# Linear attention: the norms of the small tokens divided at each wait of TensorE and dealt at half tiles, the next weights requested ahead of a norm

## The chip and the metric

The kernel runs on one NeuronCore of a Trainium2 chip. The engines are called here as the profile calls them: PE (TensorE: matmuls and transposes), DVE (VectorE), ACT (ScalarE), POOL (GpSimd) and SP (SyncE, whose queue issues most of the transfers). Each engine takes its own instructions in the order in which the built program lists them, and waits at semaphores for the others. The metric is the device time of one execution in microseconds (us), as the median of several runs.

## What is computed

One inference step of a two-layer decoder: a layer of gated linear attention (GLA), then one of differential attention, each followed by an MLP. There is a prompt of 1024 tokens, and beside it a few small tokens: 16 meta tokens and 8 samples, which the kernel keeps as one block of 32 columns. The change lies in the first layer, where the small tokens go through the whole layer beside the prompt's projections:

```python
def post_norm(x, f, g, b):
    return layer_norm(DEEPNORM_ALPHA * x + f, g, b)

def sq_relu_mlp(x, w1, w2):
    h = jax.nn.relu(x @ w1)
    return (h * h) @ w2
...
    q, k, v, lg, r = gla_project(x, w_in, w_gate, b_gate)
    s_new, o = gla_chunk(state.astype(F32), q, k, v, lg)
    return gla_output(o, r, g_norm, w_out, x.dtype), s_new
...
        x_s = post_norm(x_s, f_s, ln_mix_g[layer], ln_mix_b[layer])
...
        x_s = post_norm(x_s, sq_relu_mlp(x_s, mlp_w1[layer], mlp_w2[layer]), ln_mlp_g[layer], ln_mlp_b[layer])
```

## The kernel before

The prompt is held as high and low float32r parts, so one product is three matmuls (`mm3`, lines 206 to 208). For the heads 1 to 3, `proj(h)` (line 370) makes q, k (four tiles of 24 matmuls) and v (four tiles of 48); `decays` (435) makes the decay factors, the 32x32 blocks of At and the transposed keys (487); `advance` (494) takes a chunk's four blocks through the state (500 to 502 on PE, 504 on DVE). Then come the gates r of all heads (line 842 on), and w_out of this layer.

The small tokens are a generator beside it, `small_tokens` (779). `s_rows` (702) and `s_cols` (715) multiply by a weight matrix in pieces: two weight tiles of 1 MB are requested (lines 234 and 240, into two buffers, `swt`), then a `yield`, then 8 thin matmuls (712, 723), which the profile counts twice. The matrices come in this order: w_out of the attention, the two halves of the first MLP weight, the second MLP weight (8 pieces), and the input weight of the next layer (four pieces and two). `s_post` (726) follows w_out and the second MLP weight: an eviction by ACT (731), four transposes (734), the sum with x on DVE (740, 741), then `s_ln` (744): a sum over the columns (746), an average by a matmul (748), the subtraction (749), squares and their sum (751, 752), a second average (754), a logarithm and an exponential on ACT (758, 759), and small DVE steps up to 767.

`deal()` (819) takes the generator one `yield` further. It is called at each second tile of `proj`, at some chunks of `decays`, and once for each half of a gate tile (863), 25 times in all, so that the whole `s_post` stands between two calls.

What runs when isn't set by this order alone: the program is built by a scheduler which lists each engine's instructions by its own reckoning of what is ready, with the order of the code as the priority. The decode of the second layer (cache pages, lines 906 to 943) is code of a lower priority, which starts as soon as the small tokens' q and k rows are written.

Of the kernel before, what the change touches and what calls it, by code (L numbers as in the profile page):

```python
# [21 lines left out]
P = 128  # L22
D = 1024
T = 1024
NB = 8
# [89 lines left out]
def hybrid_step(ctx, tc, A, dbg=None, upto=9):  # L115
# [227 lines left out]
    ps = smt()  # L343
# [26 lines left out]
    def proj(h):  # L370
        hi, lo = qku if h == 0 else qk_unit(h)
        hv, lv = (w.rearrange("p (i k n) -> p i k n", i=2, n=P) for w in (hi, lo))
        for c in range(h == 0, 2):
            cs = slice(512 * c, 512 * c + 512)
            for i in range(2):
                ps = mmt()
                for k in range(NB):
                    mm3(ps, hv[:, i, k, :], lv[:, i, k, :], XH[:, k, cs], XL[:, k, cs], k == 0, k == NB - 1)
                evict_qk(c, i, ps)
                yield  # L380
        hi, lo = v0u if h == 0 else kunit(wi, 1024 + h * 256)
        hv, lv = (w.rearrange("p (k n) -> p k n", n=256) for w in (hi, lo))
        for c in range(2):
            for i2 in range(2):
                ps = mmt()
                for i in range(2):
                    t = 4 * c + 2 * i2 + i
                    for k in range(NB):
                        a = slice(t * P, (t + 1) * P)
                        mm3(ps[:, i * 256 : (i + 1) * 256], XH[:, k, a], XL[:, k, a], hv[:, k, :], lv[:, k, :], k == 0, k == NB - 1)  # L390
                S.copy(Yh[:, h, 4 * c + 2 * i2 : 4 * c + 2 * i2 + 2, :].rearrange("p i e -> p (i e)"), ps)
                yield


    def rstd_of(ssum, n, scale, pool):
# [123 lines left out]
        rr = rstd_of(gss[:, h, :], 8, 1.0 / 256, g2)  # L519
        G.tensor_tensor(Yh[:, h], Yh[:, h], bc(rr, [P, 8, 256], 2), op=ALU.mult)  # L520

    first = proj(0)
    parts = []

    def early(c):
# [173 lines left out]
        TE.transpose(ps[:, m * P : (m + 1) * P], so[:, m * P : (m + 1) * P], ident)  # L699
    V.tensor_copy(soT.rearrange("p (h m) t -> p m h t", m=2), ps[:, :256].rearrange("p (m h t) -> p m h t", m=2, h=GH))  # L700

    def s_rows(lhs, w, nk):

        ps = smt()
        for k in range(0, nk, 4):
            ts = [sload2(w, k), sload2(w, k + 2)]
            yield
            for j in (1, 0):
                for i in range(2):
                    for c in range(2):  # L710
                        o = (2 * i + c) * TS
                        TE.matmul(ps[o : o + TS, :], lhs[:, k + 2 * j + i, :], ts[j][:, i, c * 512 : (c + 1) * 512], start=k == 0 and j == 1, stop=k == nk - 4 and j == 0)
        return ps

    def s_cols(lhs, w, c0):

        ps = smt()
        for k in range(0, NB, 2):
            ts = [sload(w[x * P : (x + 1) * P, c0 : c0 + 2048]) for x in (k, k + 1)]
            yield  # L720
            for j in (1, 0):
                for c in range(4):
                    TE.matmul(ps[c * TS : (c + 1) * TS, :], lhs[:, k + j, :], ts[j][:, c * 512 : (c + 1) * 512], start=k == 0 and j == 1, stop=k == NB - 2 and j == 0)  # L723
        return ps

    def s_post(ps, ln, pool):

        sev = ps
        if pool is spool:
            sev = s2()  # L730
            S.copy(sev, ps)
        pt = smt()
        for j in range(4):
            TE.transpose(pt[:, j * P : (j + 1) * P], sev[:, j * P : (j + 1) * P], ident)

        pv = pt.rearrange("p (j q c t) -> p q c j t", j=4, q=2, c=2)
        z = pool.tile([P, NB, TS], F32, name="sz")
        for c in range(2):
            zc = z[:, 4 * c : 4 * c + 4, :]
            V.scalar_tensor_tensor(zc, sx[:, 4 * c : 4 * c + 4, :], ALPHA, pv[:, 0, c], ALU.mult, ALU.add)  # L740
            V.tensor_tensor(zc, zc, pv[:, 1, c], op=ALU.add)
        s_ln(z, ln, pool)

    def s_ln(z, ln, pool):
        s1 = pool.tile([P, TS], F32, name="ss1")
        V.tensor_reduce(s1, z.rearrange("p k t -> p t k"), op=ALU.add, axis=AX.X)
        pm = smt()
        TE.matmul(pm[:, :TS], inv, s1, start=True, stop=True)
        V.tensor_tensor(z, z, bc(pm[:, :TS], [P, NB, TS], 1), op=ALU.subtract)
        z2 = s2()[:, : NB * TS].rearrange("p (k t) -> p k t", t=TS)  # L750
        V.tensor_tensor(z2, z, z, op=ALU.mult)
        V.tensor_reduce(s1, z2.rearrange("p k t -> p t k"), op=ALU.add, axis=AX.X)
        pm = smt()
        TE.matmul(pm[:, :TS], inv, s1, start=True, stop=True)
        v = pool.tile([P, TS], F32, name="sv_")
        y = pool.tile([P, TS], F32, name="sy_")
        V.tensor_scalar(v, pm[:, :TS], EPS, None, ALU.add)
        S.activation(y, v, AF.Ln)
        S.activation(y, y, AF.Exp, scale=-0.5)

        V.tensor_tensor(v, v, y, op=ALU.mult)
        V.tensor_tensor(v, v, y, op=ALU.mult)
        V.tensor_scalar(v, v, -0.5, 1.5, ALU.mult, ALU.add)
        V.tensor_tensor(y, y, v, op=ALU.mult)
        V.tensor_tensor(z, z, bc(y, [P, NB, TS], 1), op=ALU.mult)
        V.tensor_tensor(z, z, bc(lnp[:, ln, 0, :], [P, NB, TS], 2), op=ALU.mult)
        V.tensor_tensor(sx, z, bc(lnp[:, ln, 1, :], [P, NB, TS], 2), op=ALU.add)
# [10 lines left out]

    def small_tokens():

        s_post((yield from s_rows(soT, A["gla_w_out"][0], NB)), 0, spool)
        shT = s4().rearrange("p (k t) -> p k t", t=TS)
        for half in range(2):
            ps = yield from s_cols(sx, A["mlp_w1"][0], half * 2048)
            r = s2()
            S.activation(r, ps, AF.Relu)
            V.tensor_tensor(r, r, r, op=ALU.mult)
            pt = smt()
            for j in range(4):
                TE.transpose(pt[:, j * P : (j + 1) * P], r[:, j * P : (j + 1) * P], ident)  # L790
            V.tensor_copy(shT[:, 16 * half : 16 * half + 16, :].rearrange("p (c j) t -> p c j t", j=4),
                          pt.rearrange("p (j c t) -> p c j t", j=4, c=4))
        s_post((yield from s_rows(shT, A["mlp_w2"][0], 32)), 1, spool)

        pa = yield from s_cols(sx, wd, 0)
        sqkr = s2()
        S.copy(sqkr, pa)
        tmp = s2()[:, :128].rearrange("p (n d) -> p n d", d=16)
        rope(sqkr.rearrange("p (n d) -> p n d", d=64), pa.rearrange("p (n d) -> p n d", d=64), srope, 8, tmp)
        pb = yield from s_rows(sx, wd[:, 2048:3072], NB)  # L800
        svv = s2()
        S.copy(svv[64:, :], pb[64:, :])
        S.copy(svv[:64, :], svv[64:, :])
        V.tensor_tensor(svv[:64, :], svv[:64, :], pb[:64, :], op=ALU.add)
        for c in range(2):
            hs = slice(4 * c, 4 * c + 4)
            o = 64 + c * TS
            f = lambda ap: ap.rearrange("t h d -> t (h d)")
            dma(f(A["k_rows_p"][0, 0, 0:NM, hs, :]), sqkr[o : o + NM, :])
            dma(f(A["k_rows_s"][0, :, 0, hs, :]), sqkr[o + NM : o + NM + NS, :])  # L810
            dma(f(A["v_rows_p"][0, 0, 0:NM, hs, :]), svv[c * TS : c * TS + NM, :])
            dma(f(A["v_rows_s"][0, :, 0, hs, :]), svv[c * TS + NM : c * TS + NM + NS, :])
            dma(A["qs"][:, c * 512 : (c + 1) * 512], sqkr[c * TS + NM : c * TS + NM + NS, :])

        dma(A["sxd"], sx)

    small, updates = small_tokens(), state_updates()

    def deal():
        next(small, None)  # L820

    deal()
    next(updates)
    for h in range(1, GH):
        for n, _ in enumerate(proj(h)):
            if n == 1:
                state_out()
            next(updates, None)
            if n % 2:
                deal()  # L830
        st = SM[:, h, :]
        pgs = [gate_in(h, c) for c in range(2)]
        for c in range(2):
            parts = decays(h, c, pgs[c])
            if c or h == 1:
                deal()
            st = advance(h, c, st, *parts)
        head_end(h, st)
# [3 lines left out]
    for h in range(GH):  # L842
# [3 lines left out]
        for c in range(2):  # L846
            cs = slice(512 * c, 512 * c + 512)
            sil, pts = [], []
            for m in range(2):
                ps = mmt()  # L850
                for k in range(NB):
                    ms = slice(m * P, (m + 1) * P)
                    mm3(ps, hv[:, k, ms], lv[:, k, ms], XH[:, k, cs], XL[:, k, cs], k == 0, k == NB - 1)
                s_ = silt[:, m, c, :]
                act = S.activation(s_, ps, AF.Silu).ins
                sil.append(s_)
# [658 lines left out]
    def samples():  # L1515

        sev = s2()
        dma(sev, A["srow"])
        s_post(sev, 2, hp)
        yield  # L1520

    stats = ln_stats(hp)
# [25 lines left out]
    def samples_out():  # L1548
# [7 lines left out]
        for u in range(2):  # L1556
# [4 lines left out]
            V.tensor_reduce(zc, pt.rearrange("p (j k t) -> p j t k", j=4, k=4)[:, :, 0:NS, :], op=ALU.add, axis=AX.X)  # L1561
            zc = z[:, 4 * u : 4 * u + 4, :]
            V.scalar_tensor_tensor(zc, sx[:, 4 * u : 4 * u + 4, :], ALPHA, zc, ALU.mult, ALU.add)
        s_ln(z, 3, hp)
        for u in range(2):
            ps = smt()
            for j in range(4):
# [210 lines left out]
```

## Time and profile before

| | us |
|---|---|
| median of 3 runs | 2810.68 (2808.56 to 2811.32) |
| the profiled execution | 2806.01 |
| its span, first to last instruction | 2804.1 |
| PE busy | 2722.0 |
| DVE busy | 1956.1 |
| ACT busy | 1107.8 |
| POOL busy | 1096.6 |

In the profile a time of day is counted in us from the start of the span. A busy engine is one with an instruction in it; matmuls overlap, so their durations are longer than the distance of their starts. [...] A wait is named by the instruction that ended it.

### The profile page before, as it was taken

The numbers are of one execution on the slowest core, as the hardware profiler recorded it, in microseconds if no ns is written. First come the engines' busy times: TensorE is split into PE (matmuls) and PEld (weight loads), VectorE is DVE, ScalarE is ACT, GpSimd is POOL, SyncE is SP. The second block draws the span as 40 slices with busy tenths as digits, with TensorE's granted clock in tenths as the row PEclk, the third lists the DMA queues.
The fourth block names the chain that finished last, engine by engine and source line by source line (L and its number), as shares of the span: only waits on it lengthen the run. The fifth ranks groups of instructions, "written<-read, shape, count | busy, mean of one in ns | idle before, by whom it ended". The sixth has DMA issues, their size and how long they took to land.

```text
span 2804.1 us, 52239 instructions
## 1 busy us (share of the span) xinstructions
PE 2722.0 (97%) x19849; PEld 2235.8 (80%) x19849; DVE 1956.1 (70%) x3011; ACT 1107.8 (40%) x2266; POOL 1096.6 (39%) x744
## 2 busy tenths in 40 slices
PE   9989999999999999999999999899999999999997
PEld 6867767987777777777798988777899889798985
DVE  5375453678877777777568730887648888978788
ACT  4334463152231221222242112777525546355553
POOL 2132112234343443434234222100026677686774
PEclk9999999999999999999999999999999999999998
DMA  7475544735889898888658995212144555555684
GB/s 240 161 243 213 198 162 175 268 96 178 310 315 335 304 348 303 322 313 315 241 182 315 357 372 167 58 57 77 36 121 91 102 146 113 139 124 114 133 187 99
DMA packets 275624, 562.81 MB, mean 201 GB/s; under 512 B 23510, under 2 KB 144412, under 8 KB 271276
## 3 DMA queue, kind: packets, MB, share of 16 engines
q1 hardware_dynamic: 256076, 522.75, 54.1%
q0 software_dynamic: 19296, 36.71, 8.1%
q8 instruction: 156, 2.56, 0.4%
q14 instruction: 96, 0.79, 0.1%
HBM read 533.00 MB, written 29.52 MB: 201 GB/s over the span
## 4 chain that ended last, share of the span: by engine, by line
PE 81%; DVE 9%; ACT 4%; DMA 3%; issue 2%; POOL 1%; SPq 0%; DVEq 0%; POOLq 0%; ACTq 0%
PE mmt L206 19%; PE mmt L207 18%; PE mmt L208 18%; PE smt L983 4%; PE axt L206 3%; PE axt L207 3%; PE axt L208 3%; PE smt L1354 2%; ACT as L1332 1%; PE prt L1328 1%; DVE pg L942 1%; DMA swt<-in_mlp_w 1%; PE axt L1349 1%; DVE XH L203 1%; PE smt L723 1%
## 5 line engine op out<-in xcount | busy, mean ns | idle before, releaser
L194 POOL TENSOR_TENSOR wlo<-raw,whi 128x512 fp32r<-128x512 f32 x252 | 358.4, 1435 | 708.7 <-ACT whi L193 584.9
L206 PE MATMUL mmt<-whi,XH 128*128 128x256 f32 (+1 forms) x1760 | 523.5, 300 | 1.1 <-DVE ast L1330 0.9
L207 PE MATMUL mmt<-wlo,XH 128*128 128x256 f32 (+1 forms) x1760 | 521.6, 298 | 0.4 <-POOL wlo L194 0.4
L206 PE MATMUL mmt<-XH,whi 128*128 128x512 f32 (+1 forms) x1216 | 435.5, 359 | 6.4 <-DVE Y L1053 3.0
L208 PE MATMUL mmt<-XH,wlo 128*128 128x512 f32 (+1 forms) x1216 | 431.9, 356 | 0.0
L208 PE MATMUL mmt<-whi,XL 128*128 128x256 f32 x1536 | 431.6, 284 | 0.1
L193 ACT CAST whi<-raw 128x512 fp32r<-128x512 f32 x252 | 150.3, 619 | 575.0 <-PE mmt L208 193.0
L206 PEld LDWEIGHTS mmt<-whi,XH 128*128 128x128 f32 x1760 | 330.0, 188 | 39.9 <-issue 26.1
L943 DVE TENSOR_REDUCE sc<-pg 128x16 f32<-128x1024 f32 x256 | 308.3, 1211 | 67.5 <-POOL pg L942 65.0
L207 PEld LDWEIGHTS mmt<-wlo,XH 128*128 128x128 f32 x1760 | 331.7, 188 | 15.8 <-issue 5.5
L942 DVE TENSOR_TENSOR pg<-pg,qb 128x1024 f32<-128x1024 f32 x192 | 265.7, 1391 | 63.7 <-DMA pg<-in_cache_k 57.1
L207 PE MATMUL mmt<-XL,whi 128*128 128x512 f32 x768 | 306.9, 400 | 0.0
L208 PEld LDWEIGHTS mmt<-whi,XL 128*128 128x128 f32 x1536 | 287.8, 188 | 7.3 <-issue 6.8
L206 PEld LDWEIGHTS mmt<-XH,whi 128*128 128x128 f32 x1216 | 229.3, 189 | 50.3 <-issue 7.6
L942 POOL TENSOR_TENSOR pg<-pg,qb 128x1024 f32<-128x1024 f32 x64 | 165.5, 2587 | 257.1 <-DMA pg<-in_cache_k 139.9
L208 PEld LDWEIGHTS mmt<-XH,wlo 128*128 128x128 f32 x1216 | 229.4, 189 | 35.7 <-issue 2.9
L206 PE MATMUL mmt<-whi,HH 128*128 128x512 f32 x512 | 205.4, 402 | 5.2 <-DVE Y L1167 3.5
L208 PE MATMUL mmt<-whi,HL 128*128 128x512 f32 x512 | 204.5, 399 | 0.0
L207 PE MATMUL mmt<-wlo,HH 128*128 128x512 f32 x512 | 204.0, 398 | 0.0
L1617 POOL TENSOR_TENSOR wlo<-RW,whi 128x512 fp32r<-128x512 f32 x96 | 165.8, 1766 | 61.1 <-ACT whi L1616 57.2
L1617 POOL TENSOR_TENSOR wlo<-rw,whi 128x512 fp32r<-128x512 f32 x92 | 156.9, 1774 | 81.7 <-ACT whi L1616 78.5
L207 PEld LDWEIGHTS mmt<-XL,whi 128*128 128x128 f32 x768 | 145.4, 189 | 39.3 <-issue 8.0
(438 smaller groups left out, 5720.3 us busy)
## 6 DMA issues: line engine op xcount, KB each, us to landing
pg<-in_cache_k SPq DMA_DIRECT2D x256, 512.0 KB
pg<-in_cache_v SPq DMA_DIRECT2D x256, 512.0 KB
raw<-in_mlp_w SPq DMA_DIRECT2D x164, 256.0 KB
swt<-in_mlp_w SPq DMA_DIRECT2D x32, 1024.0 KB
rw<-in_mlp_w SPq DMA_DIRECT2D x116, 256.0 KB
RW<-in_mlp_w POOLq DMA_DIRECT2D x96, 256.0 KB, 5.7
swt<-in_gla_w_in SPq DMA_DIRECT2D x12, 1024.0 KB
swt<-in_diff_w_in SPq DMA_DIRECT2D x12, 1024.0 KB
```

The costliest lines, as they stand in the source:

```text
L193: S.copy(hi[:, c], raw)
L194: G.tensor_tensor(lo[:, c], raw, hi[:, c].bitcast(F32), op=ALU.subtract)
L203: return eng.tensor_tensor(lo, src, hi.bitcast(F32), op=ALU.subtract)
L206: TE.matmul(ps, ah, bh, start=first, stop=False)
L207: TE.matmul(ps, ah, bl, start=False, stop=False)
L208: return TE.matmul(ps, al, bh, start=False, stop=last)
L723: TE.matmul(ps[c * TS : (c + 1) * TS, :], lhs[:, k + j, :], ts[j][:, c * 512 : (c + 1) * 512], start=k == 0 and j == 1, stop=k == NB - 2 a ...
L942: eng.tensor_tensor(pg, pg, qb, op=ALU.mult)
L943: return V.tensor_reduce(sc[:, n, :], pg.rearrange("p (h d) -> p h d", d=64), op=ALU.add, axis=AX.X).ins
L983: m = TE.matmul(acc[i * TS : i * TS + 16, :256], w[r, n, :], pg[r, i * 256 : (i + 1) * 256], start=n == 0, stop=n == NPG).ins
L1354: TE.matmul(out, at, v, start=j == 0, stop=j == t + 1)
L1617: G.tensor_tensor(lo[:, k, :], t, hi[:, k, :].bitcast(F32), op=ALU.subtract)
```

## The change

`s_rows` and `s_cols` get their first two weight tiles from the caller, which requests them (`rows_in`, `cols_in`) before the norm or the evaluation that stands ahead of them. Each `yield` now has a value: 0 for "a piece of weights is next", 1 for "in the middle of a chain": behind the eviction, behind each of the two sums of `s_ln`, and behind the square of a hidden half. `deal(any_)` takes the generator on if it may take any step, or if the last value was 1. `proj` yields 0 in the middle of each tile as well, and the gate loop calls `deal(False)` there; the calls that were there before stay. There are 33 steps now where there were 25. The norms of the second layer use the same functions and run through without a pause.

```diff
@@ -376,8 +376,10 @@
                 ps = mmt()
                 for k in range(NB):
                     mm3(ps, hv[:, i, k, :], lv[:, i, k, :], XH[:, k, cs], XL[:, k, cs], k == 0, k == NB - 1)
+                    if k == 3:
+                        yield 0
                 evict_qk(c, i, ps)
-                yield
+                yield 1
...
@@ -699,12 +703,21 @@
-    def s_rows(lhs, w, nk):
+    def rows_in(w, k):
+
+        return [sload2(w, k), sload2(w, k + 2)]
+
+    def cols_in(w, c0, k):
+
+        return [sload(w[x * P : (x + 1) * P, c0 : c0 + 2048]) for x in (k, k + 1)]
+
+    def s_rows(lhs, w, nk, ts):
 
         ps = smt()
         for k in range(0, nk, 4):
-            ts = [sload2(w, k), sload2(w, k + 2)]
-            yield
+            if k:
+                ts = rows_in(w, k)
+            yield 0
...
@@ -729,6 +743,7 @@
             sev = s2()
             S.copy(sev, ps)
+            yield 1
         pt = smt()
...
-        s_ln(z, ln, pool)
+        yield from s_ln(z, ln, pool)
 
     def s_ln(z, ln, pool):
         s1 = pool.tile([P, TS], F32, name="ss1")
         V.tensor_reduce(s1, z.rearrange("p k t -> p t k"), op=ALU.add, axis=AX.X)
+        yield 1
         pm = smt()
...
         V.tensor_reduce(s1, z2.rearrange("p k t -> p t k"), op=ALU.add, axis=AX.X)
+        yield 1
         pm = smt()
...
-        s_post((yield from s_rows(soT, A["gla_w_out"][0], NB)), 0, spool)
+        w1, w2 = A["mlp_w1"][0], A["mlp_w2"][0]
+        wo = A["gla_w_out"][0]
+        ps = yield from s_rows(soT, wo, NB, rows_in(wo, 0))
+        ts = cols_in(w1, 0, 0)
+        yield from s_post(ps, 0, spool)
...
-            ps = yield from s_cols(sx, A["mlp_w1"][0], half * 2048)
+            ps = yield from s_cols(sx, w1, half * 2048, ts)
+            ts = rows_in(w2, 0) if half else cols_in(w1, 2048, 0)
             r = s2()
             S.activation(r, ps, AF.Relu)
             V.tensor_tensor(r, r, r, op=ALU.mult)
+            yield 1
...
-        s_post((yield from s_rows(shT, A["mlp_w2"][0], 32)), 1, spool)
-
-        pa = yield from s_cols(sx, wd, 0)
+        ps = yield from s_rows(shT, w2, 32, ts)
+        ts = cols_in(wd, 0, 0)
+        yield from s_post(ps, 1, spool)
+        pa = yield from s_cols(sx, wd, 0, ts)
...
-    def deal():
-        next(small, None)
+    chain = [0]
+
+    def deal(any_=True):
+        if any_ or chain[0]:
+            chain[0] = next(small, 0)
...
-        for n, _ in enumerate(proj(h)):
+        n = 0
+        for whole in proj(h):
+            if not whole:
+                deal(False)
+                continue
             if n == 1:
                 state_out()
             next(updates, None)
-            if n % 2:
-                deal()
+            deal(n % 2)
+            n += 1
...
                     mm3(ps, hv[:, k, ms], lv[:, k, ms], XH[:, k, cs], XL[:, k, cs], k == 0, k == NB - 1)
+                    if k == 3:
+                        deal(False)
+                if not m:
+                    deal(False)
```

The lines behind the first hunk have other numbers in the new code: 748 and 754 are 764 and 771, 712 and 723 are 725 and 737, 452, 467, 487 and 500 to 504 are four more.

On PE at the first norm, about 189 us, before (`ss` is the sum that the average reads, `t` the decay factors of head 1):

```order
L207 MATMUL mmt<-XL_88,whi 128x512
L208 MATMUL mmt<-XH_85,wlo 128x512
L467 MATMUL axt<-t_1979 32x64 x8
L467 MATMUL axt<-t_1995 32x32 x6
L748 MATMUL smt<-ss_1645,c_inv 128x32
L467 MATMUL axt<-t_1995 32x32 x2
```

and the same place now:

```order
L207 MATMUL mmt<-XL_88,whi 128x512
L208 MATMUL mmt<-XH_85,wlo 128x512
L471 MATMUL axt<-t_1979 32x64 x8
L471 MATMUL axt<-t_1995 32x32 x6
L764 MATMUL smt<-ss_1692,c_inv 128x32
L471 MATMUL axt<-t_1995 32x32 x2
```

Nothing moved: the average stands where it stood. The rows of all five engines read alike up to the transposes of the second hidden half, at about 296 us.

On PE at the second norm, at the end of head 3, before (the first average stands further up, ahead of 19 large matmuls):

```order
L452 MATMUL axt<-t_4123 32x32 x16
L452 MATMUL axt<-t_4147 32x32 x16
L754 MATMUL smt<-ss_4416,c_inv 128x32
L206 MATMUL mmt<-XH_87,whi 128x512
L207 MATMUL mmt<-XL_89,whi 128x512
L208 MATMUL mmt<-XH_87,wlo 128x512
L487 MATMUL axt<-c_ident,t_4178 128x128 x4
L500 MATMUL axt<-Y,At_115 128x256
L501 MATMUL axt<-gS,t_4175 128x256
```

and now:

```order
L456 MATMUL axt<-t_4111 32x32 x16
L764 MATMUL smt<-ss_4517,c_inv 128x32
L456 MATMUL axt<-t_4135 32x32 x16
L491 MATMUL axt<-c_ident,t_4166 128x128 x4
L771 MATMUL smt<-ss_4517,c_inv 128x32
L504 MATMUL axt<-Y,At_115 128x256
L505 MATMUL axt<-gS,t_4163 128x256
```

The first average moved down among the tiny matmuls of At, the second from ahead of the transposes of the keys to behind them.

On DVE at the same place, before (`gAd` is the block of At, `t` the factors, `gS` the state):

```order
L752 TENSOR_REDUCE ss_4416<-s_4421 128x32
L461 COPY_PREDICATED gAd<-masks,axt 128x128 x2
L481 TENSOR_TENSOR t_4178<-gb 128x512
L479 TENSOR_TENSOR t_4175<-t_4175,gq 128x512
L461 COPY_PREDICATED gAd<-masks,axt 128x128
L483 TENSOR_TENSOR t_4178<-t_4178,gk 128x512
L461 COPY_PREDICATED gAd<-masks,axt 128x128
L757 TENSOR_SCALAR sv__4426<-smt 128x32
L461 COPY_PREDICATED gAd<-masks,axt 128x128
L761 TENSOR_TENSOR sv__4426<-sv__4426,sy__4427 128x32
```

and now:

```order
L487 TENSOR_TENSOR t_4166<-t_4166,gk 128x512
L465 COPY_PREDICATED gAd<-masks,axt 128x128
L765 TENSOR_TENSOR sz<-sz,smt 128x256
L465 COPY_PREDICATED gAd<-masks,axt 128x128
L767 TENSOR_TENSOR s<-sz 128x256
L768 TENSOR_REDUCE ss_4517<-s_4534 128x32
L774 TENSOR_SCALAR sv__4558<-smt 128x32
L778 TENSOR_TENSOR sv__4558<-sv__4558,sy__4559 128x32
```

The subtraction, the squares and their sum (749, 751, 752; now 765, 767, 768) moved from ahead of the factor of the keys (483, now 487) to behind it. The state step 504 (now 508) follows in both orders.

On SP behind the last piece of the next layer's columns, before:

```order
L809 DMA out_k_rows_p<-s_4779 16x512
L810 DMA out_k_rows_s<-s_4779 8x512
L813 DMA qs<-s_4779 8x512
L191 DMA raw<-in_gla_w_out 128x2x256 x2
L240 DMA swt<-in_diff_w_in 128x2x1024 x2
L191 DMA raw<-in_gla_w_out 128x2x256
L891 DMA ptab<-in_page_table 8x32
L895 DMA pg<-in_diff_lambda 128x256
```

and now:

```order
L835 DMA out_k_rows_p<-s_4865 16x512
L836 DMA out_k_rows_s<-s_4865 8x512
L839 DMA qs<-s_4865 8x512
L240 DMA swt<-in_diff_w_in 128x2x1024
L191 DMA raw<-in_gla_w_out 128x2x256
L240 DMA swt<-in_diff_w_in 128x2x1024
L191 DMA raw<-in_gla_w_out 128x2x256
L1218 DMA Y<-in_x_prompt 128x8x256 x4
L191 DMA raw<-in_gla_w_out 128x2x256 x2
L927 DMA ptab<-in_page_table 8x32
```

The page table (`ptab`) moved from ahead of the four loads of x_prompt to behind them and two further weight tiles.

## Rows read from the trace of the kernel before

**Rows 1.** The page: its span and PE's line.

```profile
span 2804.1 us, 52239 instructions
...
PE 2722.0 (97%) x19849; PEld 2235.8 (80%) x19849; DVE 1956.1 (70%) x3011; ACT 1107.8 (40%) x2266; POOL 1096.6 (39%) x744
```

**Rows 2.** Busy time by window (columns in its first line).

```profile
core 0: us, PE busy (x) PEld busy (x) DVE busy (x) ACT busy (x) POOL busy (x), PEclk, DMA share, GB/s
490.00:530.00 40.00, 40.00 (x342) 39.95 (x339) 24.95 (x36) 5.55 (x10) 10.82 (x7) 1.00 0.95 329
```

**Rows 3.** Timeline of PE: start, us, what; in brackets idle before, releaser.

```profile
189.01 0.64 PE L748 MATMUL smt<-ss,c_inv 128*128 128x32 f32 x2 [3.46 <-DVE ss L746]
```

**Rows 4.** Windows at the first norm.

```profile
185.00:190.00 5.00, 1.54 (x33) 1.30 (x28) 4.93 (x11) 0.42 (x2) 2.77 (x2) 0.74 0.98 325
190.00:195.00 5.00, 5.00 (x14) 3.91 (x15) 5.00 (x12) 2.03 (x6) 0.46 (x1) 0.57 0.59 172
```

**Rows 5.** Waits of PE from 296 to 426 us: total, times, longest.

```profile
PE smt L712 <- DMA swt<-in_mlp_w: 2.2, 1, 2.2
PE axt L501 <- DVE gS L504: 2.1, 2, 1.5
PE axt L500 <- ACT At L475: 1.2, 1, 1.2
...
PE axt L487 <- DVE t L483: 0.6, 1, 0.6
```

**Rows 6.** The chain of work that ended last: start, us, what.

```profile
305.41 9.49 DMA swt<-in_mlp_w
```

**Rows 7.** Windows with gaps of PE.

```profile
306.00:316.00 10.00, 7.74 (x145) 6.32 (x146) 8.37 (x21) 6.70 (x22) 0.00 (x0) 1.00 0.61 223
...
406.00:416.00 10.00, 6.78 (x184) 5.27 (x171) 5.63 (x18) 6.71 (x14) 0.00 (x0) 1.00 0.01 3
```

**Rows 8.** Timeline of PE at the end of head 3.

```profile
409.23 0.63 PE L487 MATMUL axt<-c_ident,t 128*128 128x128 f32 x4 [0.55 <-DVE t L483]
411.06 0.70 PE L500 MATMUL axt<-Y,At 128*128 128x256 f32 x2 [1.20 <-ACT At L475]
...
414.96 0.70 PE L501 MATMUL axt<-gS,t 128*128 128x256 f32 x2 [1.47 <-DVE gS L504]
```

**Rows 9.** Timeline of DVE there.

```profile
395.90 0.29 DVE L740 SCALAR_TENSOR_TENSOR sz<-sx,smt 128x128 f32<-128x128 f32 x1 [0.25 <-PE smt L734]
...
404.14 0.42 DVE L751 TENSOR_TENSOR s<-sz 128x256 f32<-128x256 f32 x1
...
405.49 0.62 DVE L752 TENSOR_REDUCE ss<-s 128x32 f32<-128x256 f32 x1
...
409.33 0.30 DVE L461 COPY_PREDICATED gAd<-masks,axt 128x128 f32<-128x128 uint8 x1
413.19 0.19 DVE L761 TENSOR_TENSOR sv__4426<-sv__4426,sy__4427 128x32 f32<-128x32 f32 x1 [3.56 <-ACT sy__4427 L759]
...
414.08 0.43 DVE L765 TENSOR_TENSOR sz<-sz,sy__4427 128x256 f32<-128x256 f32 x1
414.43 0.47 DVE L504 SCALAR_TENSOR_TENSOR gS<-gS,geb,axt 128x256 f32<-128x256 f32 x1
```

**Rows 10.** Timeline of ACT there.

```profile
408.38 1.28 ACT L758 ACT_TABLE_LOAD   x1
...
409.81 1.20 ACT L475 COPY At<-gAd 32x128 f32<-32x128 f32 x4
411.03 0.59 ACT L489 COPY t<-axt 128x512 f32<-128x512 f32 x1
411.63 1.28 ACT L759 ACT_TABLE_LOAD   x1
412.93 0.23 ACT L759 ACTIVATE sy__4427<-sy__4427 128x32 f32<-128x32 f32 x1
```

**Rows 11.** Timeline of SP's queue: the last two weight tiles.

```profile
475.23 1.23 SPq L240 DMA_DIRECT2D swt<-in_diff_w_in  x2
```

**Rows 12.** Timeline of PE: the last piece.

```profile
488.19 1.92 PE L712 MATMUL smt<-swt,sx 128*32 128x512 f32 x16
```

More of the change, by code (lines that the diff above doesn't have):

```diff
@@ L390, in proj @@
                         mm3(ps[:, i * 256 : (i + 1) * 256], XH[:, k, a], XL[:, k, a], hv[:, k, :], lv[:, k, :], k == 0, k == NB - 1)
+                    if i == 0:
+                        yield 0
                 S.copy(Yh[:, h, 4 * c + 2 * i2 : 4 * c + 2 * i2 + 2, :].rearrange("p i e -> p (i e)"), ps)
-                yield
+                yield 1
     def rstd_of(ssum, n, scale, pool):
@@ L520, in head_end @@
         G.tensor_tensor(Yh[:, h], Yh[:, h], bc(rr, [P, 8, 256], 2), op=ALU.mult)
-    first = proj(0)
+    first = (x for x in proj(0) if x)
     parts = []
@@ L700, in hybrid_step @@
     V.tensor_copy(soT.rearrange("p (h m) t -> p m h t", m=2), ps[:, :256].rearrange("p (m h t) -> p m h t", m=2, h=GH))
-    def s_rows(lhs, w, nk):
+    def rows_in(w, k):
[3 more added lines that the diff above has]
+    def s_rows(lhs, w, nk, ts):
         ps = smt()
         for k in range(0, nk, 4):
-            ts = [sload2(w, k), sload2(w, k + 2)]
-            yield
+            if k:
+                ts = rows_in(w, k)
+            yield 0
             for j in (1, 0):
@@ L713, in s_rows, with s_cols @@
         return ps
-    def s_cols(lhs, w, c0):
+    def s_cols(lhs, w, c0, ts):
         ps = smt()
         for k in range(0, NB, 2):
-            ts = [sload(w[x * P : (x + 1) * P, c0 : c0 + 2048]) for x in (k, k + 1)]
-            yield
+            if k:
+                ts = cols_in(w, c0, k)
+            yield 0
             for j in (1, 0):
@@ L787, in small_tokens @@
             V.tensor_tensor(r, r, r, op=ALU.mult)
+            yield 1
             pt = smt()
@@ L792, in small_tokens @@
                           pt.rearrange("p (j c t) -> p c j t", j=4, c=4))
-        s_post((yield from s_rows(shT, A["mlp_w2"][0], 32)), 1, spool)
-        pa = yield from s_cols(sx, wd, 0)
+        ps = yield from s_rows(shT, w2, 32, ts)
+        ts = cols_in(wd, 0, 0)
+        yield from s_post(ps, 1, spool)
+        pa = yield from s_cols(sx, wd, 0, ts)
+        wv = wd[:, 2048:3072]
+        ts = rows_in(wv, 0)
         sqkr = s2()
@@ L799, in small_tokens @@
         rope(sqkr.rearrange("p (n d) -> p n d", d=64), pa.rearrange("p (n d) -> p n d", d=64), srope, 8, tmp)
-        pb = yield from s_rows(sx, wd[:, 2048:3072], NB)
+        pb = yield from s_rows(sx, wv, NB, ts)
         svv = s2()
@@ L1518, in samples @@
         dma(sev, A["srow"])
-        s_post(sev, 2, hp)
+        for _ in s_post(sev, 2, hp):
+            pass
         yield
@@ L1563, in samples_out @@
             V.scalar_tensor_tensor(zc, sx[:, 4 * u : 4 * u + 4, :], ALPHA, zc, ALU.mult, ALU.add)
-        s_ln(z, 3, hp)
+        for _ in s_ln(z, 3, hp):
+            pass
         for u in range(2):
```

## Prediction

> **What bounds the kernel now.** I read the page first: TensorE (PE) is busy 97% of the span [rows 1]. So the time is PE's row of work plus its gaps, and I read the PE column of the windows and then its waits; what other engines do counts only where PE waits for it. The change touches the stretch in which the small tokens (one group of 32 columns: meta tokens, samples, padding) are dealt between the large matmuls, up to about 500 us. Behind it, from 490 to 530 us, PE has no gap at all [rows 2].
>
> The gap the change is aimed at is in the first layer norm of the small tokens: at 189 us PE reaches the matmul that averages (line 748) and waits 3.46 us for VectorE's sum [rows 3]. [...]
>
> **The change part by part.** On each engine the built program has as many instructions as before; only the order and a few waits differ. So nothing is paid or saved in work, and the sum is made of gaps.
>
> *Up to about 296 us.* The order on PE is row for row the same: the transposes of the first norm, its two averages and the pieces between them stand where they stood, though the code that asks for them was divided. VectorE, ScalarE, GpSimd and SyncE read the same there too. The scheduler had put this work beside other matmuls already, and the new points at which it may be dealt change nothing. The wait of 3.46 us and its slow clock stay: 0 us.
>
> *296 to 395 us.* From the transposes of the second half of the hidden layer on, the pieces of the second MLP weight move: pieces are whole more often, and each comes somewhat later. The gaps here are 2.2 us for a weight tile (line 712) and about 0.6 us in front of a line 501, the smaller of its two waits (2.1 less the 1.5 of the longest) [rows 5]. The tile that PE waits for was asked for when the piece before ended, and took 9.49 us [rows 6]. Between these two pieces the new order has three large matmuls more and 16 tiny ones fewer, some 0.3 us apart: the wait stays about 2 us. Bounds: both gaps filled (-2.8) to one more wait of that size (+2.2). I take 0, since the work between the pieces is alike.
>
> *The tail of the last head, 396 to 426 us.* Here PE has little to fill in: 3.22 us of the ten from 406 are idle [rows 7]. The second norm sits in it, in both orders, but later now. Before, its first average (line 748) stood 19 large matmuls ahead of the tiny ones, and its second (754) ahead of the transposes 487. Now the first average is among the tiny ones, and the second stands between these transposes and the first matmul of the state (500).
>  - VectorE ahead of the factor that transposes 487 wait for: before it had 749, 751 and 752 there, 0.42 + 0.42 + 0.62 = 1.46 us (749 and 751 are alike); now it has the four additions to z (740 and 741, 0.29 each) and the first sum (as 752, 0.62), 1.78 us. That is +0.3, and PE was already waiting 0.6 there [rows 5, 9].
>  - Behind that factor VectorE now does two masked copies (0.30), 749, 751 and 752: 2.06 us by durations, about 1.75 from start to start, since each starts a little before the one ahead ends. PE is free 0.6 us after 487 starts and waits some 1.0 us for it. ScalarE copies the transposes (0.59) and then the four pieces of At (1.20), in this order, so that 500 can start 2.5 us after 487 began, where it took 1.83 (409.23 to 411.06): +0.7 [rows 8 to 10].
>  - Now the logarithm and the exponential of the norm come behind the copies of At. Each has a table load of 1.28 us ahead of it and ends 0.25 us after it: 3.1 us [rows 10]. VectorE's four small steps (413.19 to 414.08: 0.9) and the state step 504 (0.47), which is queued behind them, follow. Before, the second 501 started 3.90 us after the first 500; now it is 3.1 + 0.9 + 0.5 = 4.5 us, since ScalarE finishes At just as 500 starts: +0.6 [rows 8 to 10].
>
>  The sum is 0.3 + 0.7 + 0.6 = +1.6 us. Bounds: all of the waits for 487, 500 and the larger of 501 gone (-0.6 - 1.2 - 1.5 = -3.3), to one more wait of the size that the first norm shows (+3.5). I take +1.6, since it follows the new queue order with the durations of these same steps.
>
>  [...]
>
> *The last pieces, 426 to 500 us.* One of the "any" turns falls to a norm's or a hidden half's step, so every piece of the last two matrices comes one turn, some 14 us, later. Up to now the last one ran at 488 us with its tiles requested at 475 [rows 11, 12]. Now the one before it runs there, and the last comes 81 large matmuls later. At 40 us for 342 of them that is 9.5 us [rows 2]. Its tiles can only be asked for when the piece before has freed the two buffers. The nearest row for such a pair is 9.49 us [rows 6]: it just fits, with four loads of x_prompt queued behind it rather than ahead. Cost 0 to +10 (a rival, below); I take 0.
>
> *What waits behind it.* On SyncE the page table, the rows of q and k for the samples and so the first cache pages move behind four x_prompt loads and two weight loads. The pages start some 2 to 3 us later. PE is without a gap there [rows 2] and VectorE is busy 25 of these 40 us, so I count 0 (bounds 0 to +3).
>
> **Sum.** The profiled execution took 2806.01 us (span 2804.1 [rows 1] and 1.9 around it); it becomes 2807.6. It lies 4.7 us below the median of the runs, 2810.68, so the same difference makes the median 2812.3.
>
> **The rivals.**
> 1. *The reorder is absorbed: no difference.* The chain of the tail meets other slack, the moved pieces fill as much as they open. For: 7 of 10 us of that window are PE's own work, and a few tenths either way cancel it. Time 2810.7.
> 2. *The tail's gap becomes long enough for the clock.* In the new order PE would idle some 3.5 us of the seven behind the start of 487. In the first norm a wait of 3.46 us was followed by 5 us at 0.74 and 5 us at 0.57: 0.26 x 5 + 0.43 x 5 = 3.45 us lost [rows 4]. Against it: the windows with 2.26 and 3.22 us idle kept 1.00 [rows 7]. Time 2810.68 + 1.6 + 3.45 = 2815.7. [...]
> 3. *Slower: the last weight tile comes late.* TensorE takes its row in order, so if the tiles of the last piece land after 9.5 us, all of w_out's matmuls stand behind it. If its 2 MB share the queues with two weight tiles (0.5 MB) and the x_prompt loads (4 MB), 6.5 MB at the 329 GB/s of these 40 us [rows 2] are 19.8 us, 10.3 too late: 2810.68 + 1.6 + 10.3 = 2822.6. It decides from a landing of 13.5 us on, where the sum passes 0.2%. Against it: the tiles are asked for before the x_prompt loads.
> 4. *Faster: the pieces land in the gaps.* If the waits of 2.2, 2.1, 1.2 and 0.6 us [rows 5] were all filled, the gain is 6.1: 2804.6. Against it: the 2.2 us are a transfer that starts no earlier, and the tail's chain is longer, not shorter.
>
> **How the numbers follow.** About 0.2%, 5.6 us, is what a measurement of this kernel tells from no change. Forecast 0.48, rival 1 0.20, rival 2 0.12, rival 3 0.08, rival 4 0.08, and 0.04 for what is not named, half on each side. Faster: 0.08 + 0.02 = 0.10. Slower: 0.08 + 0.02, and 0.04 from rival 2, which lies just inside the bound: 0.14. Same: 0.48 + 0.20 + 0.08 = 0.76. The range goes from 2806, the forecast with both gaps of 296 to 395 us and the tail's filled, to 2818, rival 2 with a wait of 2.2 us more; it leaves out rivals 3 and 4. The forecast's own is 2809 to 2815.
>
> **What would show it.** Right: the wait of 3.5 us at the first norm's average is still in the new trace, with the slow clock behind it; the tail from 487 to the second 501 is about 7 us where it was 5.7; PE has no gap from 430 to 560 us. Wrong: the first norm's wait is gone (the order then does not tell what runs); PE waits for a weight tile near 499 us (rival 3); the windows behind 416 us show a clock under 1.00 (rival 2); or a gap of over 2 us opens between 600 and 700 us, where VectorE takes the cache pages.

## The result and the profile after

The changed kernel takes 2821.4 us (median of 6 runs, 2818.89 to 2824.78), the kernel before 2809.6 beside it (6 runs, 2802.97 to 2811.32): the ratio is 1.0038, interval 1.0022 to 1.0054. It is slower by 11.8 us, where +1.6 was predicted; the range ended at 2818.

The page of the changed kernel (span, and PE's line), against [rows 1]:

```profile
span 2823.0 us, 52245 instructions
...
PE 2729.8 (97%) x19849; PEld 2241.8 (79%) x19849; DVE 1952.4 (69%) x3011; ACT 1107.2 (39%) x2266; POOL 1095.6 (39%) x744
```

Between these two executions lie 18.9 us: 7.8 of busy time of PE with the same number of matmuls, so slower ones, and 11.1 idle (93.2 where 82.1 were). A single execution says too much here. The program of run e8 below reads row for row like the kernel before, and that of e1 like the changed one:

```profile
span 2814.1 us, 52239 instructions
...
PE 2727.1 (97%) x19849; PEld 2240.2 (80%) x19849; DVE 1948.1 (69%) x3011; ACT 1108.2 (39%) x2266; POOL 1098.1 (39%) x744
```

```profile
span 2816.4 us, 52245 instructions
...
PE 2724.8 (97%) x19849; PEld 2239.3 (80%) x19849; DVE 1945.0 (69%) x3011; ACT 1108.5 (39%) x2266; POOL 1098.8 (39%) x744
```

So the kernel before is idle for 82.1 and 87.0 us, the changed one for 93.2 and 91.6. By the pairs' means that is +7.85 idle and +2.75 of slower matmuls, 10.6 together, which fits the medians. With two executions of each, which differ among themselves by up to 10.0 us, that is an estimate.

Waits of PE from 296 to 430 us in the changed kernel, against [rows 5]:

```profile
PE axt L456 <- issue: 2.2, 1, 2.2
PE axt L505 <- DVE gS L508: 1.9, 1, 1.9
PE smt L771 <- DVE ss L768: 1.0, 1, 1.0
...
PE smt L725 <- DMA swt<-in_mlp_w: 0.9, 2, 0.6
...
PE axt L491 <- DVE t L487: 0.6, 1, 0.6
PE axt L504 <- ACT At L479: 0.4, 1, 0.4
```

All waits of this stretch sum to 9.4 us and 10.6 in e1, against 7.8 before and 5.5 in e8: +3.4. The first row is new: PE waits 2.2 us for nothing that the profile shows. From 500 to 560 us the kernel before has no wait and e8 0.2, the changed kernel 1.2 and e1 2.1: +1.6. These two stretches hold 5.0 of the 7.85 us; the rest is spread over later stages, in which the two traces of one program already differ by as much.

The timeline of PE where the new wait stands:

```profile
315.18 1.12 PE L456 MATMUL axt<-t 128*32 128x32 f32 x96
...
318.54 0.75 PE L456 MATMUL axt<-t 128*32 128x32 f32 x63
321.49 0.21 PE L456 MATMUL axt<-t 128*32 128x32 f32 x1 [2.20 <-issue]
321.62 1.11 PE L491 MATMUL axt<-c_ident,t 128*128 128x128 f32 x4
```

PE stops in front of the last of 64 tiny matmuls of one group, whose inputs the other 63 have had. Before, no such wait stands here; e8 has one of 0.19 us among large matmuls:

```profile
323.00 0.28 PE L208 MATMUL mmt<-whi,XL 128*128 128x256 f32 x1 [0.19 <-issue]
```

The windows (columns as in [rows 2]; PEclk, the granted clock, is a share of full speed) at the first norm, around this wait, and at the tail of head 3:

```profile
185.00:190.00 5.00, 1.41 (x30) 0.78 (x28) 4.97 (x14) 1.84 (x6) 1.73 (x1) 0.81 1.05 372
190.00:195.00 5.00, 4.04 (x14) 3.24 (x15) 4.96 (x9) 1.28 (x4) 2.21 (x1) 0.50 0.88 264
306.00:316.00 10.00, 9.38 (x201) 6.91 (x202) 6.59 (x16) 5.91 (x21) 0.00 (x0) 1.00 0.60 216
316.00:326.00 10.00, 7.80 (x142) 6.96 (x137) 2.91 (x8) 4.41 (x10) 0.00 (x0) 0.83 0.42 170
406.00:416.00 10.00, 6.61 (x182) 4.97 (x181) 6.12 (x20) 5.95 (x11) 0.00 (x0) 1.00 0.01 3
416.00:426.00 10.00, 8.52 (x42) 4.93 (x43) 4.24 (x10) 3.35 (x13) 0.00 (x0) 0.83 0.45 163
```

The two windows at 0.83 each lose some 1.7 us (0.17 x 10, an estimate); by single us the clock is 0.50 from 322 to 324 and from 417 to 420, and 128x256 matmuls start 0.21 us apart at 322.75 to 324.46 where it is 0.12 ahead of the wait. Before, it was 1.00 in every ten us from 306 to 426 (two of them in [rows 7]). The second executions show the reverse: e1 keeps 1.00 in both places, and e8 has 0.83 at its tail:

```profile
316.00:326.00 10.00, 7.53 (x208) 6.77 (x211) 3.51 (x9) 4.68 (x10) 0.00 (x0) 1.00 0.51 206
416.00:426.00 10.00, 7.57 (x46) 4.67 (x46) 5.54 (x15) 4.58 (x14) 0.89 (x1) 1.00 0.58 213
```

```profile
406.00:416.00 10.00, 8.25 (x184) 6.24 (x184) 5.82 (x18) 6.70 (x14) 0.00 (x0) 0.83 0.02 3
```

### The profile page after: what moved, and what is told of

The parts are those of the page before. It is cut to its first block, busy times and chain, and to the rows that moved or that the text cites. A ratio compares the mean times of both kernels' runs of the same rounds, so it can differ in the third digit from the quotient of the medians.

```text
span 2823.0 us, 52245 instructions
## 1 busy us (share of the span) xinstructions
PE 2729.8 (97%) x19849; PEld 2241.8 (79%) x19849; DVE 1952.4 (69%) x3011; ACT 1107.2 (39%) x2266; POOL 1095.6 (39%) x744
## 3 DMA queue, kind: packets, MB, share of 16 engines
q8 instruction: 156, 2.56, 0.4%
## 4 chain that ended last, share of the span: by engine, by line
PE 76%; DVE 10%; DMA 6%; ACT 4%; issue 3%; POOL 2%; SPq 1%; DVEq 0%; POOLq 0%; ACTq 0%
PE mmt L206 17%; PE mmt L207 17%; PE mmt L208 17%; PE smt L1019 4%; PE axt L206 3%; PE axt L207 3%; PE axt L208 3%; PE smt L1390 2%; ACT as L1368 1%; DVE pg L978 1%; DMA swt<-in_mlp_w 1%; PE prt L1364 1%; POOL wlo L194 1%; DMA pg<-in_cache_k 1%; DVE Y L1728 1%
```

## The experiments

**Which part of the change acts.** e1 leaves out the early requests, e8 the division:

```diff
(e1)
-            if k:
-                ts = rows_in(w, k)
+            ts = rows_in(w, k)
...
-        ts = cols_in(wd, 0, 0)
(e8)
             S.copy(sev, ps)
-            yield 1
...
             V.tensor_tensor(r, r, r, op=ALU.mult)
-            yield 1
```

> The change without its early requests: each matrix asks for its first two weight tiles only when its turn comes, as before; the steps inside the chains and the dealing at half tiles stay. On all five engines the built program reads row for row like the changed kernel, so the early requests move nothing. Every theory expects the time of the changed kernel, +0.3 to +0.5% against before (some 2821 us); anything else would mean that programs that read alike differ by as much as the change did.

> The early requests alone: the first two weight tiles of each matrix are asked for ahead of the norm, the chains are not divided and no turn is lost. On all five engines the built program reads row for row like the kernel before. Every theory expects no difference, within 0.15%, 2806 to 2814 us. Its trace is a second one of the program before: waits that differ between the two are chance.

e1: 1.0041 (1.0026 to 1.0056). e8: 1.0000 (0.9987 to 1.0014). The early requests move nothing in the built program and give nothing. All that the change does is done by the division, and what the division does in the built program is one lost turn: up to the second MLP weight the order is the old one. That the small tokens there run later than their turns anyway, held by data and transfers, is the likely reason, but no run tests it.

**Where the lost turn costs.** e2 is the kernel before with one turn dropped at head 2, e3 with one dropped in the gate loop, e7 with one more in head 1; e4 is the changed kernel with its turn given back in the gate loop.

```diff
(e2)
-            if c or h == 1:
+            if c and h != 2 or h == 1:
                 deal()
(e3)
-            deal()
+            if h or not c:
+                deal()
(e4)
             deal()
+            if h == 0 and c == 0:
+                deal()
(e7)
-            if n % 2:
+            if n % 2 or (h == 1 and n == 0):
                 deal()
```

> The kernel before, with one call of the dealing left out (the one at the second chunk of head 2) and nothing divided: every later piece of weights comes one turn later, as in the changed kernel. Theory A, the lost turn is the whole cost: 2818 to 2824 us, like the changed kernel. Theory B, the divided norms and half tiles cost it themselves: 2810 us, like before.

> The kernel before, with one call of the dealing left out in the gate loop (first head, second chunk): the second MLP weight is asked for as before, only the pieces of the next layer's weight come one turn later, the last of them beside w_out, and the page table behind the x_prompt loads. Theory A1, the late last pieces and the later start of the cache pages cost it: 2817 to 2824 us. Theory A2, the later pieces of the second MLP weight and what they do in front of the last head's end: 2809 to 2814 us.

> The changed kernel with its lost turn given back in the gate loop (two steps at the first head's first chunk... second): the second MLP weight and the second norm stand as late as in the changed kernel, but the last six pieces stand where they stood before. Theory A1 (late last pieces, later cache pages): 2809 to 2814 us. Theory A2 (second MLP weight and the tail of the last head): 2817 to 2824 us. A sum of both: 2814 to 2818 us.

> The kernel before with one more call of the dealing, in head 1, and nothing divided: the last piece of weights runs one turn (48 large matmuls, some 14 us) earlier than before, and the second norm stands 7 and 15 large matmuls earlier. The counterpart of the dropped turn. Theory A (each turn moves the start of the cache pages, and the time follows): 2800 to 2806 us, faster than before. Theory C (before lies at the edge: earlier is hidden, later is not): 2808 to 2813 us.

e2: 1.0043 (1.0029 to 1.0058). e3: 1.0018 (1.0003 to 1.0032). e4: 1.0020 (1.0007 to 1.0033). e7: 1.0022 (1.0009 to 1.0035). A plain lost turn costs as much as the change (theory A of e2). Neither half alone does, and one turn more costs too: theories A1 and A2 each explain about half, within intervals from 0.03 to 0.33%, and "earlier is faster" falls. Equal cost is not yet equal cause: the trace of e2 has no wait of PE for nothing near 320 us, and e15 below looks whether the same shift removes both.

**What happens at 500 to 560 us.** SyncE and GpSimd there, first in the kernel before, then in the changed one:

```profile
490.18 0.30 SPq L891 DMA_DIRECT2D ptab<-in_page_table  x1
...
515.79 2.40 POOL L942 TENSOR_TENSOR pg<-pg,qb 128x1024 f32<-128x1024 f32 x1 [5.16 <-DMA pg<-in_cache_k]
```

```profile
493.31 10.28 SPq L1218 DMA_DIRECT2D Y<-in_x_prompt  x4
507.83 0.62 SPq L927 DMA_DIRECT2D ptab<-in_page_table  x1
...
528.35 2.99 POOL L978 TENSOR_TENSOR pg<-pg,qb 128x1024 f32<-128x1024 f32 x1 [25.57 <-DMA pg<-in_cache_k]
531.27 2.57 POOL L194 TENSOR_TENSOR wlo<-raw,whi 128x512 fp32r<-128x512 f32 x2
```

The first page is multiplied 12.6 us later, and w_out's low parts are queued behind its product. e5 asks for the page table ahead of the gates, e6 gives GpSimd's first two products to VectorE, e11 holds the pages behind w_out's last loads:

```diff
(e5)
+    ptab = cp.tile([NS, NPG], I32, name="ptab")
+    dma(ptab, A["page_table"])
     fmv = Y.rearrange("p (h c m t) -> p h c m t", h=GH, c=2, m=2)
(e6)
-            eng, after = (G, steps_g) if n % 4 == 3 else (V, steps_v)
+            eng, after = (G, steps_g) if n % 4 == 3 and (b or n > 7) else (V, steps_v)
(e11)
-        with tc.issue_after(gathers[-4]) if len(gathers) > 3 else nullcontext():
+        with tc.issue_after(gathers[-4] if len(gathers) > 3 else rawq[-1]):
...
-                if side and (n == 4 if scaled else n < 12):
+                if side and (n == 4 if scaled else 8 <= n < 20):
```

> The changed kernel with the page table in a tile of a pool that is open earlier, and requested ahead of the gates instead of behind the four x_prompt loads. PE's, ScalarE's and GpSimd's orders are unchanged; on SyncE the first page requests move up. In the changed kernel the table was asked for at 506 to 508 us instead of 490, the first cache page was asked for at 517 to 519 instead of 506, GpSimd stood 25.8 us in front of its product with a page, and PE then waited 2 us near 541 for low parts of w_out queued behind that product. Theory P (the table's place is what delays the pages): the first page is multiplied before 520 us, PE's idle time from 500 to 680 us falls by 2 to 5 us, and the time by 3 to 8, to 2814 to 2819 us. Theory Q (the x_prompt loads and the late weight tiles fill the queue, and pages are late with or without the table): 2819 to 2824 us, as the changed kernel.

> The changed kernel with the first two cache pages that GpSimd multiplies given to VectorE, so that nothing but w_out's low parts stands in GpSimd's queue from 500 to 560 us. Theory P1 (PE's wait there is GpSimd's queue, held by a page that comes late): no idle time of PE from 500 to 560 us (1.2 to 2.1 in the changed kernel), 2818 to 2821 us, since the later cache pages still come late. Theory P2 (the low parts are late because their own transfers are): the idle time stays 1 to 2.5 us, 2820 to 2824 us.

> The changed kernel with the requests for the cache pages held behind w_out's last transfers on SyncE's queue (one page is still ahead), and the first steps of the decode dealt eight tiles later. In the changed kernel w_out's loads between 530 and 545 us took 5.5 to 7.6 us from request to use, where they took 3.9 before, while the burst of first pages moved from 505 to 520 us onto them. Theory H (the burst of pages is what delays them): these loads take about 4 us again and PE's idle time from 500 to 560 us falls from 1.2 to 2.1 us to under 0.4, although the decode starts later still. Theory I (the late last piece itself delays the chain of w_out's loads): it stays over 1 us. For the whole time this is a gain of 1.5 us against what the later decode costs: 2815 to 2830 us.

e5: 1.0013 (0.9997 to 1.0030); the first page is as late as ever and PE waits 1.3 us, so theory P falls. Its interval overlaps that of e1, so it is not shown to be faster than the changed kernel. e6: 1.0032 (1.0018 to 1.0045), with 1.5 us idle in the stretch: not GpSimd's queue. e11: 1.0046 (1.0031 to 1.0061), and PE is never idle there. The window in the changed kernel, then in e11:

```profile
500.00:560.00 60.00, 58.77 (x487) 56.16 (x486) 35.72 (x48) 6.89 (x12) 16.81 (x11) 1.00 0.84 283
```

```profile
500.00:560.00 60.00, 60.00 (x508) 58.42 (x507) 19.85 (x37) 6.84 (x12) 12.25 (x10) 1.00 0.65 216
```

Theory H fits this wait: the first pages, 12 us late, now come beside w_out's loads. A load of w_out asked for at 534.4 us is used 6.5 us later in the changed kernel; before it took 3.8 (from 529.3), in e11 3.0 (from 531.9). But e11 also deals the decode's first steps later, so its two edits are not parted. In e4, whose last pieces and pages stand near their old places (first product at 518.5 us), PE is never idle here either. The whole time does not fall with e11: what it gains here it loses later.

**The wait for nothing.** In seven traces (changed, e1, e4 to e7, e11) PE stands 2.2 to 2.9 us in front of its instruction number 6338, matmuls, weight loads and its separate semaphore instructions counted from the start; the same burst of tiny matmuls stands there in all of them. The page's line of DMA queues says `q8 instruction: 156, 2.56, 0.4%` (packets, MB, share): 16 KB each, and PE's 39928 instructions (2 x 19849, and 230 for semaphores and the like) over 156 are 256 for each (in e13, 40182 over 157), and 64 bytes an instruction by these figures. In the changed kernel such a packet ends at 320.2 us, 1.3 before PE goes on; in the other six it is 1.3 to 1.5. e9 puts 32 tiny matmuls (128 instructions) at the start, while PE waits for its first load; e13, e14 and e16 put 64, 16 and 48 there; e10, e17 and e18 are the kernel before with 32, 48 and 16; e15 is e2 with 32.

```diff
+    ps = smt()
+    for k in range(32):
+        TE.matmul(ps[:TS, :TS], ones[:, :TS], ones[:, :TS], start=True, stop=True)
     x_split(0, 0)
```

> The changed kernel with 32 tiny matmuls on TensorE at the very start, while it waits for the first load (128 instructions more, the result is read by nothing). In six traces of five programs TensorE stood 2.2 to 2.9 us near 321 us in front of its instruction number 6338, with no wait for another engine, and went on 1.3 us after a 16 KB load of instructions had ended; in five of these six the clock fell to 0.50 for 3.4 us right there. Theory F (it ran out of instructions, at a border of such a load): the border now lies 128 instructions earlier in the work, among slower ones; the gap near 321 us is gone or elsewhere, and the time falls by 2 to 4 us, to 2817 to 2819 us. Theory G (something in that place of the work itself makes the gap): the gap stays in front of the same tiny matmul, and the time stays at 2821 to 2824 us.

> The kernel before with the same 32 tiny matmuls at its start, as a control of what the addition itself costs or gives. Theory F: 2808 to 2813 us, as before, if the moved borders meet no burst of tiny matmuls; up to 4 us more if one does, and then its trace has a gap of over 2 us with nothing waited for.

> The changed kernel with 64 tiny matmuls at its start, 256 instructions: as many as a 16 KB load holds if an instruction has 64 bytes, which is an estimate that this run tests. Theory F (the borders of the instruction loads against the work set the cost): the borders fall on the same work as without the addition, the gap of 2.2 to 2.9 us in front of the last of a burst of tiny matmuls near 320 us is back, and the time with it: 2818 to 2823 us, where 128 instructions gave 2811. Theory J (tiny matmuls at the start help in another way, by the clock or the start of the loads): 2808 to 2813 us.

> The changed kernel with 16 tiny matmuls at its start, 64 instructions; TensorE's order behind them is unchanged to the row. Theory F: the border falls 64 instructions earlier, still inside the burst of 63 tiny matmuls near 320 us: a gap of about 2 us stands in the middle of that burst, and the time is 2815 to 2822 us. Theory J: no gap, 2808 to 2813 us.

> The kernel before with one turn dropped, and the 32 tiny matmuls at its start. Without them it took +0.43%, though its trace has no gap at a border near 320 us. Theory F in its wide form (borders anywhere set the cost of a moved order): 2809 to 2814 us. Its narrow form (only the gap near 320 us, which this order lacks): 2818 to 2824 us, as without them.

> The changed kernel with 48 tiny matmuls at its start, 192 instructions. Theory F: the border near 320 us falls into the end of the burst of 96 tiny matmuls in front, of a block that begins with slower ones: no gap or one under 1 us, 2809 to 2815 us. With e9 (128) and e13 (256) it shows whether the time follows the place of the border or the number of tiny matmuls.

> The kernel before with 48 tiny matmuls at its start, 192 instructions: the control for e16, which took +0.62% and so went against theory F. If the addition itself costs at this number (theory K: the place of every instruction against its loads moves the time of any order by some tenths of a per cent), before takes +0.2 to +0.6% too: 2816 to 2827 us. If it is the changed order that costs (theory L), before stays at 2808 to 2814 us, as with 32 tiny matmuls.

> The kernel before with 16 tiny matmuls at its start, 64 instructions: the control for e14, which took +0.13%. Theory K: anything from -0.2 to +0.4%. Theory L: 2808 to 2814 us.

| instructions added | before | changed | changed less before |
|---|---|---|---|
| 0 | 1.0000 (e8) | 1.0041 (e1) | +0.41% |
| 64 | 0.9992 (0.9976 to 1.0008) | 1.0013 (0.9996 to 1.0030) | +0.21% |
| 128 | 1.0001 (0.9985 to 1.0017) | 1.0005 (0.9989 to 1.0021) | +0.04% |
| 192 | 1.0061 (1.0038 to 1.0084) | 1.0062 (1.0039 to 1.0084) | +0.01% |
| 256 | | 1.0051 (1.0034 to 1.0068) | |

Each difference is uncertain by 0.2 to 0.3%. e15 took 1.0027 (1.0012 to 1.0042). The place in e9:

```profile
314.87 1.11 PE L459 MATMUL axt<-t 128*32 128x32 f32 x96
...
318.23 0.76 PE L459 MATMUL axt<-t 128*32 128x32 f32 x64
318.93 0.66 PE L494 MATMUL axt<-c_ident,t 128*128 128x128 f32 x4
```

and in e13:

```profile
320.43 3.64 PE L728 MATMUL smt<-swt,s 128*32 128x512 f32 x16 [4.23 <-DMA swt<-in_mlp_w]
326.01 1.07 PE L459 MATMUL axt<-t 128*32 128x32 f32 x96
...
329.32 0.76 PE L459 MATMUL axt<-t 128*32 128x32 f32 x64
331.67 0.65 PE L494 MATMUL axt<-c_ident,t 128*128 128x128 f32 x4 [1.59 <-issue]
```

With 128 more the same bursts run through. With 256 the wait is back one matmul further on in the work, at number 6595; with 64 a wait of 0.9 us, which the profile puts down to VectorE, stands in the middle of the burst, at number 6340 (here too a 16 KB packet ends 1.4 us before PE goes on); with 192 there is none. The other traces agree: behind the start, PE has 21 waits of over 0.15 us for which the profile shows no cause, in 14 of the 20 traces, and every one stands at a number that leaves 194 or 195 when divided by 256. The 0.19 us of e8 are at number 6338 as well. So this wait follows the instruction number, in steps of 256, as many as there are for each packet, and a packet ends 1.3 to 1.5 us before PE goes on. That fits theory F, that PE ran out of instructions at such a border: the traces show the place and the packet, and that PE had none left is inferred from them. Why PE waits at this border, and not at nearly all the others, is not shown.

As the whole account of the time theory F falls. 192 has no such wait near 320 us and is the slowest; and e2, a plain lost turn, has no such wait anywhere and costs +0.43%; with the 128 instructions that bring the changed order to +0.05% it still costs +0.27% (e15), though these two intervals overlap. By e17 the kernel before is as slow with 192 as the changed one, as theory K expected: instructions without use at the start move either order by up to 0.6%. That they do so by these borders is not shown: with 192, waits of PE without a cause sum to 0.6 and 0.7 us in a whole trace. In both kernels with 192, PE has some 3 us of waits near 2330 to 2357 us that are absent with none or 64 added (with 128 they stand near 2655 in both). How 192 comes to cost 17 us is open.

**An attempt to do better.** e12 starts the small tokens later and deals at every tile of heads 2 and 3:

```diff
-            deal(n % 2)
+            deal(True if h > 1 else n % 2 and n > 6)
...
-            if c or h == 1:
+            if c or h <= 2:
```

> An attempt to do better: the changed kernel with the small tokens started three turns later in head 1, so that the first norm's averages stand 24 large matmuls further down on TensorE, and with a turn at every tile of heads 2 and 3 and one more in head 2's decays, so that the last piece runs 48 large matmuls earlier than in the kernel before. If the first norm's wait (3.5 us and 3.4 us of slow clock) goes and the end comes as early as it is listed: 2800 to 2807 us. If the wait only moves: 2810 to 2815 us. If the order puts bursts or gaps elsewhere, as each moved turn did so far: 2813 to 2820 us.

1.0077 (1.0052 to 1.0101): slower than all others. Its waits of PE up to 500 us:

```profile
PE smt L725 <- DMA swt<-in_mlp_w: 8.8, 2, 6.7
PE axt L471 <- DVE t L428: 5.6, 2, 3.8
```

The pieces then come closer together than their tiles. No version was measurably faster than the kernel before.

## Why the prediction was wrong

**Up to 296 us: right.** PE still stands at the first average, 3.94 us, and the windows behind 185 us show 0.81 and 0.50, as [rows 3, 4] did:

```profile
190.96 0.64 PE L764 MATMUL smt<-ss,c_inv 128*128 128x32 f32 x2 [3.94 <-DVE ss L761]
```

**296 to 395 us: this step failed.** It took 0, since the work between the pieces was "alike", and priced only waits for transfers and engines. The move of the pieces took the thin matmuls from between the tiny ones, which now run as 96 and 64 in a row, and PE stood for nothing that the profile shows in front of number 6338: 2.2 us, and 2.5 in e1. The waits for weight tiles stayed about as they were (2.2 us before and 1.2 in e8; 0.9 and 1.8 in the changed order). Idle time of PE from 296 to 400 us is 2.8 and 2.0 before, 3.8 and 5.0 now: +2.0 where 0 was forecast. That lies just inside the stated bounds (+2.2), by luck, since they were made from waits of [rows 5], none of which has this cause. In the profiled execution the granted clock fell behind the wait (0.83 over ten us), some 1.7 us more; in e1, with the longer wait, it did not. By the page there are 256 instructions for each of 156 packets, and of all these borders the changed kernel's trace has such a wait behind the start at two only: 1.2 us at 231 us, which e1 does not have, and the 2.2 us in front of number 6338.

**The tail of head 3: right in mechanism and size.** The rows that answer to [rows 8]:

```profile
409.77 0.63 PE L491 MATMUL axt<-c_ident,t 128*128 128x128 f32 x4 [0.62 <-DVE t L487]
411.36 0.41 PE L771 MATMUL smt<-ss,c_inv 128*128 128x32 f32 x2 [0.96 <-DVE ss L768]
412.18 0.70 PE L504 MATMUL axt<-Y,At 128*128 128x256 f32 x2 [0.41 <-ACT At L479]
...
416.54 0.96 PE L505 MATMUL axt<-gS,t 128*128 128x256 f32 x2 [1.94 <-DVE gS L508]
```

From the transposes to 504 it is 2.41 us (2.5 predicted), to the second 505 from there 4.36 (4.5); the average waits 0.96 (1.0). The 0.3 in front of the transposes was 0.07. Together +1.1 us of the predicted +1.6. In the second pair of executions, e8 and e1, the same distances grew by +0.6 and +0.5.

**The clock in the tail (rival 2): partly.** In the profiled execution it did fall behind the tail (0.83 from 416 to 426 us), at 1.7 us instead of 3.45; in e1, whose program reads the same, it did not, and in e8, which reads as before, it did. So it is not a property of the new order alone.

**The last pieces: right.** No wait for a tile stands near 499 us, and from 430 to 500 PE has no gap; rival 3 did not come.

**What waits behind them: mis-sized.** The pages come 12.6 us later, not 2 to 3: the four x_prompt requests, priced at nothing, take SyncE 10.3 us in front of what the pages need, and asking for the table alone earlier (e5) changes nothing. The cost is 1.2 to 2.1 us from 500 to 560 us, inside the bounds (0 to +3) but not 0. The gap that was to be looked for between 600 and 700 us was the wrong place.

**The sum.** With 64, 128 and 192 instructions added to both kernels the change costs +0.21, +0.04 and +0.01%, on average 2.4 us, uncertain by some 4: that agrees with the forecast of +1.6, and would agree with nothing or with 6 us as well. What the prediction had no term for is that the time of either order hangs on how many instructions stand ahead of it, by up to 17 us with 192. At the place where the two kernels were compared this went against the change. Of the +11.8 the runs show 3.4 us of idle time from 296 to 430 and 1.6 from 500 to 560, and some 3 in slower clock; the remaining 4 are not located. Nor is it shown why e9 wins back all of the cost, some 10 us, where the wait that it removes and the clock behind it were worth 4.

## What to carry over

A reorder that counts out to a microsecond or two can still land ten microseconds off. Part of that here was a wait of 2.2 us for nothing that the profile shows, behind a burst of tiny matmuls and at a step of 256 instructions; for the rest no cause was found, and with 128 or 192 instructions ahead of both kernels the difference was gone. Before a change of some tenths of a per cent is credited or blamed, run both versions with several numbers of matmuls without use ahead of the work. And when a generator deals out work, count whether a finer division takes turns from what follows: here it took one, and the early requests did not reach the built program.

## What the runs showed of the hardware

- TensorE stood 2.2 to 2.9 us without a releaser in front of its instruction number 6338 in seven traces, behind a burst in which some 160 tiny matmuls and 18 large ones took some 4 us. All 21 waits of TensorE over 0.15 us without a releaser behind the start, in 20 traces, stand in steps of 256 instructions, as many as the page of the changed kernel gives for each 16 KB packet of queue q8 (39928 over 156).
- 128 instructions without use at the start took a kernel from +0.41% to +0.05%, and 192 took another from 0 to +0.61%.
- Two executions of programs that read alike row for row (before and e8) differed by 10.0 us in span (2804.1 and 2814.1), 5.1 of it in PE's busy time with the same matmuls.
